# Two of the up weights' four sums, and the first four sums of each pair of values, made by GpSimd instead of VectorE

## The chip, the cores and the metric

The kernel runs on one core of one Trainium2 chip. The core has TensorE (PE, matmuls, with a row of its own for weight loads, PEld), VectorE (DVE), ScalarE (ACT), GpSimd (POOL) and SyncE (SP, which here issues the DMAs). All engines run their own instruction stream in a fixed order and wait for each other by semaphores. The metric is the device time of one execution in microseconds; lower is better.

## The reference

One layer of an encoder over 16 learned meta tokens and 256 tokens (L = 272) of width 2048, all in float32. The layer has an input projection, two groups of attention heads, an output projection with a residual, and a gated MLP with 5632 inner columns. The change touches the MLP alone:

```python
def conv_glu(x, w_gate, w_up, conv_w, conv_b, w_down):
    g = x @ w_gate
    u = x @ w_up
    gp = jnp.pad(g, ((0, 0), (pad, pad), (0, 0)))
    gc = conv_b
    for i in range(CONV_W):
        gc = gc + conv_w[i] * gp[:, i:i + L]
    return (jax.nn.silu(gc) * u) @ w_down
```

`x` is the normalised hidden state. Meta tokens are dropped at the end, so the up product and the down product need 256 tokens only, and the gate product 258.

## The kernel before

**Products in three.** The matmuls run on float32 data rounded to a shorter form (fp32r). To keep the precision, every operand is split into a high part and a low part: `hi` is the rounded value, `lo` is the difference. A product is then the sum of three matmuls: hi by hi, hi by lo, lo by hi (lines 605 to 608 for most weights, line 278 for the products of the scheme below). Weights come from HBM in pieces of up to 128 x 1024 (`raw`, five tiles and a sixth, `more_raw`, in the MLP). For each piece ACT writes the high part (`whi<-raw`, line 238) and DVE the low part (`wlo<-raw,whi`, line 242, a subtraction of two tensors). There are four `whi` and four `wlo` tiles, so the splits can be at most four pieces ahead of TensorE. `split_hi` and `split_lo` (lines 549 to 579) take the pieces in the one order in which TensorE uses them.

**The scheme of seven products.** For some blocks of the weights the kernel uses a scheme of the Strassen-Winograd kind: a product of 2 x 2 blocks from seven block products instead of eight. For the up weights this is done for six groups of four column tiles (`QUADS = (4,10,16,22,28,36)`), called quads; each needs 8 row pairs (`RowPair`), each of them one load of 128 x 1024 and four sums of its quarters of 256 columns, made in `weight_sums` (line 529): one instruction of 512 columns that makes two of them, and then two of 256, each of which needs the one before. The sums go to a second `raw` tile. A row pair has two pieces: one with raw quarters (512 + 256 columns) and one with the four sums (1024 columns). Both are split as above. The event `summed[1]`, set after the last sum, releases the split of the second piece.

**Values.** Gate tiles pass the convolution and SiLU (`gated`); `tile_up` or, for quads, `quad_out` and `quad_value` multiply the up product with the gate. `finish_value` (line 1783) splits the value for the down product. When both tiles of a pair are done, `value_sums` (line 1800) makes four sums of 128 columns in place, one after the other, then splits the result (`split_plain`: ACT high, DVE low) into the one tile `sums` and saves it by DMA to DRAM (`save_sums`); the down stage, which uses the scheme too, reads it back (`s_down<-sums` in the profile). `hl_sums` calls the same function, with a `place` or before the MLP's buffers exist (`act is None`), for sums of the hidden state. The values live in twelve tiles `mt`.

**What sets the order.** Nothing is ordered by hand. Each engine's instruction stream comes from a planner that runs when the kernel is built (`Flow`, line 111): the code is written as generators, each `yield "dve", ns` asks for an engine for a planned time, and the planner always issues the request that can start first; equal ones go by priority. Helpers give the planned times: `TT` is a tensor-tensor operation on DVE (line 240, 68 + 1.04 ns per column), `PTT` the same on POOL (line 264, 90 + 2.7 ns per column), `ACT` an activation (line 234). The planner knows of no effect of one engine on another's speed. The result is a static order for every engine, SP's DMA issues included. So a changed planned time can change the order of all that follows.

**The MLP's order of work** (`work`, lines 427 to 479): first tiles 0 to 3 plainly, then for each quad its gate tiles, the scheme's pieces mixed with the gate and up pieces of the next tiles, and the end of these. The down stage comes behind, with the scheme for half of its output columns and plain products for the others. In it POOL adds the residual (`PTT`).

Of the kernel before, what the change touches and what calls it, by code (L numbers as in the profile page):

```python
# [12 lines left out]
ALU = mybir.AluOpType  # L13
# [192 lines left out]
def encoder_block(ctx: ExitStack, tc: tile.TileContext, io):  # L206
    nc = tc.nc
# [14 lines left out]
    def size(ap):  # L222
        n = 1
        for s in ap.shape[1:]:
            n *= s
        return n
# [13 lines left out]
    def TT(out, a, b, op):  # L240
        yield "dve", 68 + 1.04 * size(out)
        nc.vector.tensor_tensor(out, a, b, op)  # L242
# [20 lines left out]

    def PTT(out, a, b, op):
        yield "pool", 90 + 2.7 * size(out)
        nc.gpsimd.tensor_tensor(out, a, b, op)  # L266

    def cost(l, r):
# [17 lines left out]
    def meta_copies(row, lo, n=P):  # L286

        out = row[:n, L : L + 3 * CW].rearrange("p (i x) -> p i x", i=3)[:, :, :N_META]
        src = row[:n, SEQ:L]
        his = out[:, :2] if lo == 2 else out[:, ::2]  # L290
        yield from ACT(his.bitcast(F32R), repeated(src, 2), AF.Copy)
        yield from PTT(out[:, lo].bitcast(F32R), src, out[:, 0], ALU.subtract)
# [4 lines left out]
    def one(slots):  # L297
        (t,) = yield slots, 1
        return t
# [141 lines left out]
    for w, f in enumerate(QUADS):  # L441
# [6 lines left out]
        for i in range(KC // 2):  # L448
            r = RowPair(io["w_up_s"][w][i], i, PW // 4)
# [7 lines left out]
        for i, u in enumerate(scheme):  # L457
            a, b = (j * len(middle) // len(scheme) for j in (i, i + 1))
# [9 lines left out]
    for g in range(FC // 2):  # L468
        r = RowPair(io["w_down_s"][g], g, PW // 2)
# [34 lines left out]
    def load_pair(r):  # L504
        if r.of == "up":
            r.raw, r.sums = yield raws, 2
        else:
            r.raw = yield from one(quarters)
        def load_S():
            if r.near:  # L510
                r.ev_S = ev_near[r.g]
                return
            r.S = yield from one(s_parts)
            src, saved = saved_sums[r.of][r.g]
            yield saved
            yield "sp", 600
            load(r.S, src, r.ev_S, nc.sync)

        if r.of == "up":
            yield from load_S()  # L520
        for a in range(0, 4 * r.q, PW):
            yield "sp", 600
            ev = r.loaded if a + PW == 4 * r.q else Event()
            load(r.raw[:, a : a + PW], r.src[:, a : a + PW], ev, nc.sync)
        if r.of == "down":
            yield from load_S()
        fl.spawn(weight_sums(r), (lambda: 0) if r.of == "up" else 2)

    def weight_sums(r):
        yield r.loaded  # L530
        if r.of == "down":
            r.sums = yield from one(sums4)
        t, raw, q = r.sums, r.raw, r.q
        yield from TT(t[:, : 2 * q], raw[:, q : 3 * q], raw[:, : 2 * q], ALU.subtract)
        fl.set(r.summed[0])
        yield from TT(t[:, 2 * q : 3 * q], raw[:, 2 * q : 3 * q], t[:, :q], ALU.subtract)
        yield from TT(t[:, 3 * q :], t[:, 2 * q : 3 * q], raw[:, 3 * q :], ALU.subtract)
        fl.set(r.summed[1])
        r.used("raw")

# [359 lines left out]
    def rope(t, n, out, tmp):  # L900

        half = ROPE // 2
        for i in range(P // half):
            yield "sp", 600
            j = i ^ 1
            swapped = Event()
            load(tmp[i * half : (i + 1) * half, :n], t[j * half : (j + 1) * half], swapped, nc.sync)
        yield from PTT(out, t, const("cos", n), ALU.mult)
        yield swapped
        yield from TT(tmp[:, :n], tmp[:, :n], const("sin", n), ALU.mult)  # L910
        yield from PTT(out, out, tmp[:, :n], ALU.add)
# [67 lines left out]
    for h in range(HEADS):  # L979
        t = apool.tile([P, 2, NT], F32R, name=f"ob{h}")  # L980
        ob.append((t[:, 0, :], t[:, 1, :]))
        t = apool.tile([P, 2, NT], F32R, name=f"oa{h}") if h < 6 else hl[KC - HEADS + h]
# [6 lines left out]
    def split_plain(hi, lo, src):  # L989
        yield from ACT(hi, src, AF.Copy)  # L990
        yield from TT(lo, src, hi.bitcast(F32), ALU.subtract)
# [734 lines left out]
    act = mts = None  # L1726
# [56 lines left out]
    def finish_value(f, u):  # L1783
        fl.put(mts, gates[f])
        u_ = u[:, :SEQ]
        if f >= FC - KC:
            yield ev_far[(f - FC + KC) // 2]
        yield from ACT(act[:, f, 0, :], u_, AF.Copy)
        yield from TT(act[:, f, 1, :], u_, act[:, f, 0, :].bitcast(F32), ALU.subtract)
        fl.set(ev_act[f])  # L1790
        values[f] = u
        if f ^ 1 in values:
            yield from value_sums(
                *saved_sums["down"][f // 2], *(values[i][:, :SEQ] for i in (f & ~1, f | 1))
            )
            for i in (f & ~1, f | 1):
                fl.put(mts, values[i])

    values = {}
    def value_sums(dst, saved, a, b, place=None):  # L1800

        (A11, A21), (A12, A22) = ((t[:, :P], t[:, P:SEQ]) for t in (a, b))

        yield from TT(A22, A21, A22, ALU.add)
        yield from TT(A21, A11, A21, ALU.subtract)
        yield from TT(A11, A22, A11, ALU.subtract)
        yield from TT(A12, A12, A11, ALU.subtract)
        parts = place
        if place is None:
            parts = yield from one(combined)  # L1810
        hl_ = parts.bitcast(F32R).rearrange("p (i t) -> p i t", i=4)
        for i, t in enumerate((a, b)):
            yield from split_plain(hl_[:, i], hl_[:, 2 + i], t)
        fl.spawn(save_sums(dst, saved, parts, place is None))

    def save_sums(dst, saved, parts, release):
        yield "sp", 600
        load(dst, parts, saved, nc.sync)
        fl.cur.t = saved.time
        if release:  # L1820
            fl.put(combined, parts)
# [4 lines left out]
    def hl_sums():  # L1826
        for i in range(KC // 2):
            for k in (2 * i, 2 * i + 1):
                yield ev_h[k]
            if i >= EARLY:  # L1830
                yield ev_mlp
            v = yield from one(raws)
            ab = [v[:, j * SEQ : (j + 1) * SEQ] for j in range(2)]
            for k, t in zip((2 * i, 2 * i + 1), ab):
                yield from ACT(t, hT[k][:, :SEQ], AF.Copy, scale=vec("g_ffn", k))
            fl.set(ev_gained[i])
            yield from value_sums(*saved_sums["up"][i], *ab, near[i])
            if i >= EARLY:
                fl.set(ev_near[i])
            fl.put(raws, v)  # L1840
# [370 lines left out]
```

## Time and profile before

| | |
|---|---|
| runs, median (lowest to highest) | 1108.89 us (1108.64 to 1109.74) |
| profiled execution: span, first to last instruction | 1106.7 us |
| PE busy | 1100.6 us, 99% |
| weight loads busy | 1061.8 us, 96% |
| DVE busy | 990.8 us, 90% |
| ACT busy | 735.1 us, 66% |
| POOL busy | 140.0 us, 13% |
| clock of TensorE granted | 1.000 |
| moved by DMA | 239.41 MB, 216 GB/s on the mean |

The profiled execution has no time of its own beside its span; what lies around the span is seen only as its distance to the runs' median. The gate and up stage lies between about 394 and 870 us of the span, the down stage behind it.

How to read the rows. A row of instructions in order of time begins with the start and the duration in us, then engine, line, operation, the tile written, an arrow, the tiles read, the shapes, and a count; in brackets stands how long the engine had been idle and what ended it. A row of a group ends with busy time in us and the mean duration in ns, and after the bar the idle time in front of the group's instructions. Reported durations of consecutive DVE instructions overlap by some hundredths of a microsecond. Matmuls are pipelined: a matmul of 258 columns is shown as 0.28 us long, while the next starts 0.12 us after it.

### The profile page before, as it was taken

The numbers are of one execution on the slowest core, as the hardware profiler recorded it, in microseconds if no ns is written. First come the engines' busy times: TensorE is split into PE (matmuls) and PEld (weight loads), VectorE is DVE, ScalarE is ACT, GpSimd is POOL, SyncE is SP. The second block draws the span as 40 slices with busy tenths as digits, with TensorE's granted clock in tenths as the row PEclk, the third lists the DMA queues.
The fourth block names the chain that finished last, engine by engine and source line by source line (L and its number), as shares of the span: only waits on it lengthen the run. The fifth ranks groups of instructions, "written<-read, shape, count | busy, mean of one in ns | idle before, by whom it ended". The sixth has DMA issues, their size and how long they took to land.

```text
span 1106.7 us, 22544 instructions
## 1 busy us (share of the span) xinstructions
PE 1100.6 (99%) x8414; PEld 1061.8 (96%) x8414; DVE 990.8 (90%) x1837; ACT 735.1 (66%) x1470; POOL 140.0 (13%) x202
## 2 busy tenths in 40 slices
PE   9999999999999999999999999999999999999998
PEld 9999999999999999999999999999999988888888
DVE  8979888888878989999999999988988999999984
ACT  8788979798647776656666565665565565655663
POOL 3211222121433400000000000000000011100114
PEclk9999999999999999999999999999999999999999
DMA  9553434444665796657667577777688787777772
GB/s 323 199 172 124 148 127 151 139 163 134 230 188 161 207 343 229 198 181 243 224 193 230 179 248 241 238 229 244 203 275 299 260 299 250 251 258 266 281 249 77
DMA packets 72374, 239.41 MB, mean 216 GB/s; under 512 B 8136, under 2 KB 12744, under 8 KB 72264
## 3 DMA queue, kind: packets, MB, share of 16 engines
q1 hardware_dynamic: 71976, 237.69, 63.8%
q8 instruction: 66, 1.08, 0.4%
q14 instruction: 44, 0.36, 0.1%
q10 hardware_dynamic: 288, 0.27, 0.1%
HBM read 219.44 MB, written 17.83 MB: 214 GB/s over the span
## 4 chain that ended last, share of the span: by engine, by line
PE 90%; ACT 4%; DVE 3%; issue 1%; DMA 1%; POOL 0%; DVEq 0%; POOLq 0%; ACTq 0%
PE bank L278 24%; PE bank L606 18%; PE bank L607 18%; PE bank L608 18%; PE bank L1870 6%; PE bank L1871 3%; PE bank L284 2%; ACT whi L238 1%; ACT scr L238 1%; DVE wlo L242 1%; DVE scr L250 1%; DMA raw<-in_w_cq 1%; ACT qraw L238 0%; ACT bank L238 0%; DVE cols L258 0%
## 5 line engine op out<-in xcount | busy, mean ns | idle before, releaser
L238 ACT ACTIVATE whi<-raw 128x512 fp32r<-128x512 f32 (+2 forms) x479 | 358.1, 764 | 173.2 <-PE bank L607 83.5
L242 DVE TENSOR_TENSOR wlo<-raw,whi 128x512 fp32r<-128x512 f32 (+2 forms) x479 | 414.9, 885 | 43.2 <-ACT whi L238 42.1
L606 PE MATMUL bank<-hl,whi 128*128 128x258 f32 (+2 forms) x1528 | 438.5, 287 | 0.1
L607 PE MATMUL bank<-hl,whi 128*128 128x258 f32 (+2 forms) x1528 | 433.7, 284 | 0.0
L608 PE MATMUL bank<-hl,wlo 128*128 128x258 f32 (+2 forms) x1528 | 433.0, 283 | 0.2 <-DVE wlo L242 0.2
L608 PEld LDWEIGHTS bank<-hl,wlo 128*128 128x128 f32 x1528 | 290.1, 190 | 0.9 <-DVE wlo L242 0.7
L607 PEld LDWEIGHTS bank<-hl,whi 128*128 128x128 f32 x1528 | 289.6, 190 | 0.1
L606 PEld LDWEIGHTS bank<-hl,whi 128*128 128x128 f32 x1528 | 288.6, 189 | 0.5 <-ACT scr L238 0.3
L238 ACT ACTIVATE whi<-quarters 128x1024 fp32r<-128x1024 f32 x88 | 81.5, 950 | 64.8 <-PE bank L1870 46.0
L278 PE MATMUL bank<-whi,act 128*128 128x256 f32 (+1 forms) x420 | 111.5, 317 | 0.0
L1870 PE MATMUL bank<-act,whi 128*128 128x512 f32 x308 | 110.1, 397 | 0.0
L242 DVE TENSOR_TENSOR wlo<-quarters,whi 128x1024 fp32r<-128x1024 f32 x88 | 99.4, 1156 | 10.8 <-ACT whi L238 10.2
L266 POOL TENSOR_TENSOR mt<-mt,mt 128x256 f32<-128x256 f32 x7 | 6.8, 979 | 652.4 <-ACT mt L238 652.4
L1871 PE MATMUL bank<-act,wlo 128*128 128x256 f32 x308 | 86.4, 281 | 0.0
L278 PE MATMUL bank<-whi,sin 128*128 128x512 f32 (+1 forms) x272 | 83.5, 355 | 0.0
L278 PEld LDWEIGHTS bank<-whi,act 128*128 128x128 f32 x420 | 74.1, 189 | 5.7
L1870 PEld LDWEIGHTS bank<-act,whi 128*128 128x128 f32 x308 | 57.8, 188 | 13.9
L278 PE MATMUL bank<-whi,hl 128*128 128x256 f32 x288 | 66.5, 280 | 0.0
L278 PE MATMUL bank<-wlo,act 128*128 128x256 f32 (+1 forms) x210 | 66.3, 315 | 0.0
L238 ACT ACTIVATE whi<-more_raw 128x1024 fp32r<-128x1024 f32 (+2 forms) x46 | 44.1, 962 | 24.4 <-PE bank L607 9.9
L1871 PEld LDWEIGHTS bank<-act,wlo 128*128 128x128 f32 x308 | 58.1, 189 | 1.6
L278 PEld LDWEIGHTS bank<-whi,sin 128*128 128x128 f32 x272 | 49.5, 188 | 7.7
(278 smaller groups left out, 1947.9 us busy)
## 6 DMA issues: line engine op xcount, KB each, us to landing
raw<-in_w_gate SPq DMA_DIRECT2D x83, 512.0 KB, 5.0
raw<-in_w_in SPq DMA_DIRECT2D x52, 512.0 KB, 3.9
raw<-in_w_up_s SPq DMA_DIRECT2D x44, 512.0 KB, 4.9
quarters<-in_w_down_s SPq DMA_DIRECT2D x44, 512.0 KB, 6.9
raw<-in_w_up SPq DMA_DIRECT2D x34, 512.0 KB, 5.5
raw<-in_w_out SPq DMA_DIRECT2D x32, 512.0 KB, 4.0
raw<-in_w_down SPq DMA_DIRECT2D x32, 512.0 KB, 5.2
s_down<-sums SPq DMA_DIRECT2D x22, 512.0 KB, 4.1
```

The costliest lines, as they stand in the source:

```text
L238: nc.scalar.activation(out, in_, f, **kw)
L242: nc.vector.tensor_tensor(out, a, b, op)
L250: nc.vector.scalar_tensor_tensor(out, a, s, b, op0, op1)
L266: nc.gpsimd.tensor_tensor(out, a, b, op)
L278: nc.tensor.matmul(o, l, r, start=start, stop=stop)
L284: nc.tensor.transpose(o, i, ident[:n, :n])
L606: nc.tensor.matmul(ps, whi, xhi, start=start, stop=False)
L607: nc.tensor.matmul(ps, whi, xlo, start=False, stop=False)
L608: nc.tensor.matmul(ps, wlo, xhi, start=False, stop=stop)
L1870: nc.tensor.matmul(ps, whi, x, start=start, stop=False)
L1871: nc.tensor.matmul(ps[:, :n], wlo, x[:, 0, :], start=False, stop=stop)
```

## The change

`SLOW` is a new helper: a tensor-tensor operation on POOL, planned at 150 + 4.1 ns per column. It is used at two places. In `weight_sums` the second and the third instruction (256 columns each) go to POOL where the row pair is one of the up weights; the first (512 columns) stays on DVE, and the down weights' sums stay on DVE. In `value_sums` the four sums of 128 columns go to POOL where they are sums of values (the MLP's `act` exists and no `place` is given); the sums of the hidden state stay on DVE. That is 48 row pairs x 2 and 22 value pairs x 4 instructions. Nothing that is computed changes.

```diff
+    def SLOW(out, a, b, op):
+        yield "pool", 150 + 4.1 * size(out)
+        nc.gpsimd.tensor_tensor(out, a, b, op)
+
...
         yield from TT(t[:, : 2 * q], raw[:, q : 3 * q], raw[:, : 2 * q], ALU.subtract)
         fl.set(r.summed[0])
-        yield from TT(t[:, 2 * q : 3 * q], raw[:, 2 * q : 3 * q], t[:, :q], ALU.subtract)
-        yield from TT(t[:, 3 * q :], t[:, 2 * q : 3 * q], raw[:, 3 * q :], ALU.subtract)
+        sub = SLOW if r.of == "up" else TT
+        yield from sub(t[:, 2 * q : 3 * q], raw[:, 2 * q : 3 * q], t[:, :q], ALU.subtract)
+        yield from sub(t[:, 3 * q :], t[:, 2 * q : 3 * q], raw[:, 3 * q :], ALU.subtract)
         fl.set(r.summed[1])
...
-        yield from TT(A22, A21, A22, ALU.add)
-        yield from TT(A21, A11, A21, ALU.subtract)
-        yield from TT(A11, A22, A11, ALU.subtract)
-        yield from TT(A12, A12, A11, ALU.subtract)
+        op = TT if act is None or place is not None else SLOW
+        yield from op(A22, A21, A22, ALU.add)
+        yield from op(A21, A11, A21, ALU.subtract)
+        yield from op(A11, A22, A11, ALU.subtract)
+        yield from op(A12, A12, A11, ALU.subtract)
```

## The prediction

> **What bounds the kernel now.** I read the page first, then busy time by stretches of the gate and up stage, then what TensorE waits for there, and last single instructions in order of time. The page:
>
> ```profile
> span 1106.7 us, 22544 instructions
> ## 1 busy us (share of the span) xinstructions
> PE 1100.6 (99%) x8414; PEld 1061.8 (96%) x8414; DVE 990.8 (90%) x1837; ACT 735.1 (66%) x1470; POOL 140.0 (13%) x202
> ```
>
> The terms below are laid against this execution, whose span is 1106.7 us. The shown runs have a median of 1108.89 us, 2.2 us more, and I add the change to that median. The stage cut at the ends of its six quads (a quad is the four up tiles that one scheme makes; I call the stretch from one to the next a round):
>
> ```profile
> 433.20:500.00 66.80, 66.80 (x562) 66.80 (x562) 61.45 (x110) 40.51 (x61) 0.00 (x0) 1.00 0.62 203
> 500.00:566.90 66.90, 66.90 (x563) 66.90 (x562) 64.24 (x120) 41.33 (x66) 0.00 (x0) 1.00 0.65 213
> 566.90:633.70 66.80, 66.80 (x561) 66.80 (x561) 64.05 (x120) 41.09 (x66) 0.00 (x0) 1.00 0.66 213
> 633.70:700.60 66.90, 66.90 (x563) 66.90 (x562) 64.20 (x123) 40.88 (x65) 0.00 (x0) 1.00 0.70 228
> 700.60:790.50 89.90, 89.90 (x755) 89.90 (x754) 80.02 (x144) 52.88 (x82) 0.00 (x0) 1.00 0.72 236
> 790.50:868.00 77.50, 77.50 (x650) 77.50 (x649) 69.27 (x120) 47.68 (x72) 0.00 (x0) 1.00 0.79 272
> ```
>
> The columns are the stretch, its length, then busy time of PE, weight load, DVE, ACT and POOL, the clock, and the DMA share. PE is never idle, and rounds of one shape take the same time and the same number of matmuls. POOL does nothing. DVE is busy 64.2 of 66.9 us, 2.7 us idle. That PE's busy time is no artefact of pipelining shows in what its groups waited for between 400 and 860 us:
>
> ```profile
> L606 PE MATMUL bank<-hl,whi 128*128 128x258 f32 (+1 forms) x934 | 264.7, 283 | 0.0
> L607 PE MATMUL bank<-hl,whi 128*128 128x258 f32 (+1 forms) x935 | 264.5, 283 | 0.0
> L608 PE MATMUL bank<-hl,wlo 128*128 128x258 f32 (+1 forms) x935 | 263.5, 282 | 0.0
> ```
>
> So the stage is bound by TensorE. DVE's work is hidden, however near to full it is. But it is hidden narrowly. A weight piece is usable when DVE has written its `wlo`; I set the end of that against the first matmul that reads it and call the distance the lead. The first and the last of the eight pieces of the stage with a lead under 0.5 us, and between them one that a weight sum holds up:
>
> ```profile
> 510.29 1.22 DVE L242 TENSOR_TENSOR wlo<-raw,whi 128x1024 fp32r<-128x1024 f32 x1
> ```
> ```profile
> 511.94 0.28 PE L608 MATMUL bank<-hl,wlo 128*128 128x258 f32 x1
> ```
> ```profile
> 517.15 1.06 ACT L238 ACTIVATE whi<-raw 128x1024 fp32r<-128x1024 f32 x1 [3.26 <-DVE raw L242]
> ```
> ```profile
> 517.69 0.42 DVE L242 TENSOR_TENSOR more_raw<-raw,more_raw 128x256 f32<-128x256 f32 x1
> 518.15 0.42 DVE L242 TENSOR_TENSOR more_raw<-more_raw,raw 128x256 f32<-128x256 f32 x1
> 518.49 1.22 DVE L242 TENSOR_TENSOR wlo<-raw,whi 128x1024 fp32r<-128x1024 f32 x1
> ```
> ```profile
> 520.08 0.28 PE L278 MATMUL bank<-wlo,act 128*128 128x256 f32 x1
> ```
> ```profile
> 716.75 1.23 DVE L242 TENSOR_TENSOR wlo<-raw,whi 128x1024 fp32r<-128x1024 f32 x1 [1.17 <-ACT whi L238]
> ```
> ```profile
> 718.29 0.28 PE L608 MATMUL bank<-hl,wlo 128*128 128x258 f32 x1
> ```
>
> The leads are 511.94 - (510.29 + 1.22) = 0.43, 520.08 - (518.49 + 1.22) = 0.37 and 718.29 - (716.75 + 1.23) = 0.31 us. At 517.15 ACT had stood idle 3.26 us for the last sum of a row pair: the work that now goes to POOL lies on the path with no slack.
>
> **The change, part by part.** *What leaves DVE.* The groups of round 500 to 566.9, two sums for each of 8 row pairs and four for each of 3 value pairs:
>
> ```profile
> L242 DVE TENSOR_TENSOR raw<-raw,raw 128x256 f32<-128x256 f32 x8 | 3.4, 421 | 0.2
> ...
> L242 DVE TENSOR_TENSOR mt<-mt,mt 128x128 f32<-128x128 f32 x9 | 2.4, 282 | 0.0
> ...
> L242 DVE TENSOR_TENSOR more_raw<-more_raw,raw 128x256 f32<-128x256 f32 x4 | 1.7, 421 | 0.1
> L242 DVE TENSOR_TENSOR more_raw<-raw,more_raw 128x256 f32<-128x256 f32 x4 | 1.7, 419 | 0.0
> ...
> L242 DVE TENSOR_TENSOR mt<-mt 128x128 f32<-128x128 f32 x3 | 0.8, 282 | 0.0
> ```
>
> That is 3.4 + 1.7 + 1.7 = 6.8 us for 16 sums of 256 columns and 2.4 + 0.8 = 3.2 us for 12 of 128: 10.0 us of a round. By itself this is worth nothing, since no matmul waits for DVE; it could pay only as longer leads.
>
> *What it costs to have POOL run beside DVE.* The stage shows no POOL, so the price is from the output projection, where it adds tensors of 258 columns: two POOL instructions and two DVE instructions of one form, the first DVE one beside POOL, the second alone; then a POOL one that met DVE at work, and the narrow form:
>
> ```profile
> 324.71 0.74 POOL L266 TENSOR_TENSOR res<-res,scr 128x258 f32<-128x258 f32 x1 [4.01 <-DVE scr L242]
> ```
> ```profile
> 324.88 1.11 DVE L242 TENSOR_TENSOR wlo<-raw,whi 128x512 fp32r<-128x512 f32 x1
> ```
> ```profile
> 325.41 1.09 POOL L266 TENSOR_TENSOR res<-res,scr 128x258 f32<-128x258 f32 x1
> ```
> ```profile
> 326.97 0.68 DVE L242 TENSOR_TENSOR wlo<-raw,whi 128x512 fp32r<-128x512 f32 x1
> ```
> ```profile
> 350.94 3.09 POOL L266 TENSOR_TENSOR kr<-kr,scr 128x258 f32<-128x258 f32 x1 [4.29 <-ACT scr L238]
> ```
> ```profile
> L266 POOL TENSOR_TENSOR p<-p 128x16 fp32r<-128x16 f32 x40 | 13.1, 330 | 52.9 <-ACT p L238 44.7 <-PE bank L607 3.5 <-PE bank L608 3.5
> ```
>
> The two engines hold each other up: DVE's 0.68 became 1.11 us, 0.43 lost to one POOL sum; POOL's 0.74 became 1.09, and 3.09 where DVE went on without a gap. A sum of 256 thus frees 0.42 us of DVE and takes up to 0.43 back. For 128 columns no POOL row exists. Its DVE loss lies between 0 (POOL runs in DVE's idle time) and 0.43; I take 0.43 x 128/258 = 0.21, by width. Per round: 16 x 0.43 + 12 x 0.21 = 6.9 + 2.5 = 9.4 us against 10.0 freed; with both ends, 0 to 12.0. DVE is as full as before: the relief is taken back by the contention. With 12.0 it would be 64.2 + 2.0 = 66.2 of 66.9, still not over.
>
> The Trainium skill, page "SBUF — State Buffer", section "SBUF: two separate sides", says that GpSimd and a DVE instruction with two SBUF inputs share a port pair under an exclusive lock, held for the whole instruction. The trace agrees that they exclude each other, but only 0.43 of POOL's 0.74 us was lost. The sum by the rule is that of the second rival.
>
> *The longer chain.* The second and third sum depend on each other, and the ACT split of the sums piece waits for the third. On DVE, back to back, they took 518.15 + 0.42 - 517.69 = 0.88 us. On POOL they take 2 x 0.74 = 1.48 if free, 0.74 + 1.09 = 1.83 if they alternate with DVE, 2 x 3.09 = 6.18 if DVE starves both. I take 1.83, since at 96% of DVE's time a free POOL is the exception and two starved sums another: 0.95 us later. Where DVE itself put splits between the sums POOL may instead be earlier. Behind the waiting split on ACT are the next pieces' splits, in a fixed order, and behind DVE's `wlo` of that piece all its later work; so 0.95 us reaches the next pieces, and the lead pays for it. Eight pieces have leads of 0.31 to 0.43, 3.1 us together: 8 x 0.95 - 3.1 = 4.5 us of TensorE stall. Sixteen more lie between 0.72 and 1.16; those under 0.95 give 1.4 us. Sum 5.9. Ends: 0 (relief and delay cancel), and 48 row pairs x 0.95 = 45.6 us if no lead covered any of it.
>
> *Value sums.* A 128-wide POOL sum, between 0.33 and 0.74 us by the rows for 16 and 258 columns, is about 0.33 + 0.41 x 112/242 = 0.52; a chain of four 2.1 us against 4 x 0.28 = 1.1. What hides it is that these parts are saved for the down stage; the extra 1.0 us holds ACT's split of the sums, two `mt` tiles and the single `sums` tile. The save is a DMA in SP's order with loads behind it:
>
> ```profile
> 565.21 0.33 SPq L488 DMA_DIRECT2D s_down<-sums  x1
> 565.58 0.43 SPq L488 DMA_DIRECT2D raw<-in_w_up_s  x1
> ```
>
> The next load goes out 0.37 us behind the save, so a save late by 1.0 us makes it late too. I take 0 for it, as DVE is freed at the same place by 3.2 us a round; if that cover is gone it is 1 us for each of the 6 rounds, within the range. No DMA is added or removed. The planner prices the new sums at 150 + 4.1 ns per column, so all queues behind them are ordered anew, and it does not know that DVE is slowed; it can gain no more than TensorE's idle time in the stage, which rounds to 0.0, and lose some single waits of the 3.26 us kind. I take 0, since TensorE's order of products is fixed, and leave both to the range.
>
> Sum: 1108.9 + 5.9 = 1114.8, say 1115 us.
>
> **The rivals.** *First, no stall: not slower.* The chain starts on POOL as soon as the first sum is done, where DVE now has other splits in between (the 3.26 us wait), and the chain's 0.95 us is met by DVE's 10.0 freed before its 9.4 is taken back. It decides if the chain is later by less than the 0.4 us of the tightest leads. Time: 1108.9, 1108 to 1111. For it: the balance on DVE is within 1 us; against: the tight pieces lie just in the scheme, where POOL works.
>
> *Second, the lock is the bound.* If each POOL sum takes its whole duration from DVE, a round loses 16 x 0.74 + 12 x 0.52 = 18.1 us against 10.0, and the surplus 8.1 exceeds the 2.7 idle by 5.4; the stage is 434.8 / 66.9 = 6.5 rounds, so +35, 1144 us. If all idle time of the six stretches (434.8 - 403.2 = 31.6) could be used it is 6.5 x 8.1 - 31.6 = +21, 1130 us. For it: the 3.09 row, and leads near zero; against: the 0.43 row. This is where the skill's rule named above leads.
>
> *Third, faster.* It needs matmul waits to remove. TensorE's gaps in the stage round to 0.0, so only the way into the down stage and its new order of loads could give more than 0.2%. Time about 1106.
>
> **How the numbers follow.** 0.2% (2.2 us) is about what a measurement of this kernel can tell from no change. Local stalls, 1111.2 to 1126: 0.48. No stall: 0.27. Lock-bound, over 1126: 0.20. Faster by more: 0.05. So slower 0.68, same 0.27, faster 0.05. The range 1108 to 1138 leaves out the faster case, the lower edge of the second and the upper third of the lock case. The likeliest case's own range is 1111 to 1126.
>
> **What would show it.** In the profile after: POOL busy about 16 x 0.74 + 12 x 0.52 = 18 us a round or more, with sums over 1 us; DVE's 1024-wide `wlo` longer than 1.22 on the mean, and DVE's busy time in the rounds about as before, with 10 us less of sums; the rounds longer than 66.9 us, with PE idle behind `wlo`, at row pairs' sums pieces; ACT's wait for a weight sum put down to POOL. Wrong if the rounds stay at 66.9 (first rival), if DVE's busy time falls by 5 us or more a round (no contention), or if rounds grow by 4 us or more (second).

## The result, and the profile after

The changed kernel takes 1111.42 us (1111.09 to 1112.19, 13 runs) where the kernel before takes 1109.12 (1108.44 to 1109.74, 13 runs, on the same chip): a ratio of 1.0022 with a 95% interval of 1.0014 to 1.0031. It is slower by 2.3 us. The prediction was 1115 us, slower by 5.9.

The head of the page of the changed kernel:

```profile
span 1109.5 us, 22685 instructions
## 1 busy us (share of the span) xinstructions
PE 1102.0 (99%) x8414; PEld 1062.6 (96%) x8414; DVE 982.7 (89%) x1653; ACT 733.2 (66%) x1470; POOL 346.3 (31%) x386
```

The span has grown by 2.8 us. POOL is busy 206 us longer, DVE 8 us less. With the same sums made by nobody (relief alone, below) DVE is busy 48 us less between 400 and 870 us (387.4 instead of 435.4), so most of what was taken off DVE has come back as longer instructions. The PE groups of the changed kernel between 400 and 860 us (lines 611 to 613 are the former 606 to 608):

```profile
L611 PE MATMUL bank<-hl,whi 128*128 128x258 f32 (+1 forms) x927 | 262.7, 283 | 0.0
L612 PE MATMUL bank<-hl,whi 128*128 128x258 f32 (+1 forms) x927 | 262.3, 283 | 0.0
L613 PE MATMUL bank<-hl,wlo 128*128 128x258 f32 (+1 forms) x927 | 261.9, 283 | 1.7 <-DVE wlo L242 1.7
```

TensorE, which had waited for nothing here, now waits 1.7 us for DVE's `wlo`. This is three waits, one in each of three rounds. A modelled matmul end hides part of each, so the starts tell more. The first one, in the order of PE's instructions, and the DVE instruction that it waited for:

```profile
511.84 0.29 PE L612 MATMUL bank<-hl,whi 128*128 128x258 f32 x1
512.66 0.39 PE L613 MATMUL bank<-hl,wlo 128*128 128x258 f32 x1 [0.53 <-DVE wlo L242]
```
```profile
511.39 1.22 DVE L242 TENSOR_TENSOR wlo<-raw,whi 128x1024 fp32r<-128x1024 f32 x1
```

512.66 - 511.84 = 0.82 us from one start to the next, where 0.12 is usual: a loss of 0.70. The `wlo` ends at 512.61; its lead is 0.05 us, and so it was exactly this piece that held TensorE. Counted in PE's order, the matmul at 512.66 is the 4194th of 8414, and the 4194th of the kernel before is the one at 511.94, for which the prediction read a lead of 0.43 us. The matmuls of the other two stalls started there at 578.79 and 645.65, with leads of 0.42 and 0.43. With two smaller slips in the same round (0.11 us each) the loss is 0.92 us, and three rounds make 2.8, the whole growth of the span. The other rounds lose nothing.

POOL's sums in the stage, by form (the mean duration in ns is the second number behind the bar), and the longest of them:

```profile
L270 POOL TENSOR_TENSOR raw<-raw,raw 128x256 f32<-128x256 f32 x70 | 99.1, 1415 | 173.4 <-DVE raw L242 139.4 <-ACT whi L238 25.3 <-DMA raw<-in_w_gate 6.3
L270 POOL TENSOR_TENSOR mt<-mt,mt 128x128 f32<-128x128 f32 x64 | 54.8, 867 | 53.6 <-DVE act L242 52.1
```
```profile
511.61 5.48 POOL L270 TENSOR_TENSOR raw<-raw,raw 128x256 f32<-128x256 f32 x1 [3.88 <-DVE raw L242]
```

A thing that came late in front of the stalls shows best in the second of the three rounds: SP's save of a value pair and the load just ahead of it, and ACT's next instruction on the `sums` tile.

```profile
568.75 0.33 SPq L492 DMA_DIRECT2D raw<-in_w_gate  x1
```
```profile
s_down<-sums SPq DMA_DIRECT2D x1, 512.0 KB, 5.0
```
```profile
574.46 0.42 ACT L238 ACTIVATE sums<-mt 128x256 fp32r<-128x256 f32 x1 [2.99 <-DMA s_down<-sums]
```

The save goes out at 569.35, 4.1 us later than in the kernel before (565.21), and the second row is the DMA view's line for it: 5.0 us to landing. There is one `sums` tile, so the split of the next pair can begin only when the save has landed, at 574.38. ACT stood for 2.99 us in front of that split. Its stream is in a fixed order: the weight splits behind it, which could have run, stood too. In the kernel before no such split waited in this round.

That this wait is what made the `wlo` late can't be read from the trace. DVE, which writes the `wlo`, never came to rest in front of the first stall (columns as in the prediction: length, PE, PEld, DVE, ACT, POOL):

```profile
490.30:512.60 22.30, 21.83 (x183) 21.62 (x181) 22.30 (x37) 14.68 (x27) 15.23 (x18) 1.00 0.51 173
```

DVE was busy for all of these 22.30 us, so in this order an earlier `whi` would not have made the piece earlier. What set its time is what stands in front of it in DVE's stream, and how long each of these instructions takes beside POOL. One of them stands just ahead of the piece:

```profile
510.79 0.68 DVE L242 TENSOR_TENSOR raw<-raw 128x512 f32<-128x512 f32 x1
```

Nor is the save the only thing that ACT waits for. Between 394 and 870 us it waited 7.1 us for saves by the profile's count, and for POOL's row sums more than that:

```profile
ACT whi L238 <- POOL raw L270: 30.3, 13, 3.5
```

### The profile page after: what moved, and what is told of

It is laid out like the page before. It is cut to its first block, busy times and chain, and to the rows that moved or that the text cites. A ratio compares the mean times of both kernels' runs of the same rounds, so it can differ in the third digit from the quotient of the medians.

```text
span 1109.5 us, 22685 instructions
## 1 busy us (share of the span) xinstructions
PE 1102.0 (99%) x8414; PEld 1062.6 (96%) x8414; DVE 982.7 (89%) x1653; ACT 733.2 (66%) x1470; POOL 346.3 (31%) x386
## 4 chain that ended last, share of the span: by engine, by line
PE 87%; DVE 6%; ACT 3%; DMA 2%; issue 1%; POOL 0%; DVEq 0%; SPq 0%; ACTq 0%; POOLq 0%
PE bank L282 22%; PE bank L613 18%; PE bank L611 18%; PE bank L612 18%; PE bank L1876 6%; PE bank L1877 3%; DVE wlo L242 3%; PE bank L288 2%; ACT whi L238 1%; DVE scr L250 1%; ACT scr L238 1%; DMA raw<-in_w_up_s 1%; DMA raw<-in_w_cq 1%; DVE raw L242 0%; DVE sums L242 0%
## 5 line engine op out<-in xcount | busy, mean ns | idle before, releaser
L242 DVE TENSOR_TENSOR wlo<-raw,whi 128x512 fp32r<-128x512 f32 (+2 forms) x472 | 442.7, 955 | 55.8 <-ACT whi L238 54.2
L270 POOL TENSOR_TENSOR raw<-raw,raw 128x256 f32<-128x256 f32 x70 | 99.1, 1415 | 173.4 <-DVE raw L242 139.4
L270 POOL TENSOR_TENSOR mt<-mt,mt 128x128 f32<-128x128 f32 x66 | 56.9, 873 | 53.8 <-DVE act L242 52.1
L242 DVE TENSOR_TENSOR wlo<-more_raw,whi 128x1024 fp32r<-128x1024 f32 (+2 forms) x53 | 54.7, 1041 | 2.5 <-ACT whi L238 1.4
```

## The experiments

Each is timed in several rounds beside the kernel before, on one chip for each group of four. Three theories: A, a value pair's save is late and ACT waits for it at the head of its queue; B, the row pairs' sums come late from POOL (the prediction's step); C, the lock between DVE and POOL as such.

| run | median, us | ratio to before, 95% |
|---|---|---|
| changed kernel | 1111.42 | 1.0022 [1.0014, 1.0031] |
| values only | 1111.09 | 1.0020 [1.0011, 1.0028] |
| rows only | 1110.43 | 1.0013 [1.0004, 1.0022] |
| all, save planned later | 1111.20 | 1.0024 [1.0015, 1.0033] |
| all, price doubled | 1126.49 | 1.0158 [1.0145, 1.0172] |
| rows only, save planned later | 1109.35 | 1.0003 [0.9994, 1.0012] |
| values only, save planned later | 1109.16 | 1.0003 [0.9994, 1.0011] |
| all, chain cut, save planned later | 1108.63 | 0.9997 [0.9989, 1.0006] |
| relief alone | 1109.02 | 1.0001 [0.9992, 1.0010] |
| all, chain cut | 1111.27 | 1.0021 [1.0011, 1.0030] |
| all, measured price, save planned later | 1111.04 | 1.0019 [1.0010, 1.0028] |
| all, price doubled, save planned later | 1123.75 | 1.0132 [1.0116, 1.0147] |
| before, save planned later | 1108.83 | 1.0000 [0.9991, 1.0010] |

**One half of the change at a time.** Values only:

```diff
-        sub = SLOW if r.of == "up" else TT
+        sub = TT
```

> Only the values' sums are made by GpSimd; the row pairs' sums are back on VectorE. Three theories. A, the late save: a value pair's parts are saved late, the single sums tile comes free late, and ScalarE, in order, waits about 3 us for it with weight splits behind. B, the row pairs' chain: the split of the sums piece waits for GpSimd's third sum (the prediction's step). C, the lock: VectorE is slowed by GpSimd as a whole. A expects the three stalls of about 0.9 us to stay, 1110.5 to 1112 us where before has 1109.1. B expects no stall, 1108.7 to 1109.5. C expects a loss by the number of columns, 88 x 128 of 35840, about a third of 2.3 us: 1109.9.

Rows only:

```diff
-        op = TT if act is None or place is not None else SLOW
+        op = TT
```

> Only the row pairs' sums are made by GpSimd; the values' sums are back on VectorE. A expects no stall, 1108.7 to 1109.5 us. B expects the whole loss, 1111 to 1112. C expects two thirds of it, about 1110.6.

Either half alone costs nearly as much as both: 2.3 and 1.6 us, which do not add up to 2.3. No theory had expected that of both halves; B is wrong on the values, A's expectation for the rows is missed, and C, which comes close for the rows (1110.6), is missed for the values (1109.9). Both runs stall at the same three matmuls as the changed kernel. The trace of each has the wait, ACT's at the `sums` tile, first with the values' sums on POOL, then with the rows':

```profile
507.16 0.42 ACT L238 ACTIVATE sums<-mt 128x256 fp32r<-128x256 f32 x1 [2.52 <-DMA s_down<-sums]
```
```profile
510.01 0.42 ACT L238 ACTIVATE sums<-mt 128x256 fp32r<-128x256 f32 x1 [1.49 <-DMA s_down<-sums]
```

With the values' sums back on DVE the save waits still; only shorter. So the save is late in the new order of instructions whichever half brings that order about. With the rows on POOL the wait reaches DVE just in front of the piece that held TensorE:

```profile
510.46 0.43 DVE L242 TENSOR_TENSOR sums<-mt,sums 128x256 fp32r<-128x256 f32 x1 [0.69 <-ACT sums L238]
```

With the values on POOL it doesn't, in the first and the third stall: there DVE was idle for at most 0.04 us at a time in the 22 us in front of them, as in the changed kernel.

**The wait for the save taken away.** In `save_sums` the planner believes that the tile is free when the load model says so. Told that it comes 3 us later, it orders ACT's weight splits ahead of the next pair's split, and DVE's order changes with it:

```diff
-        fl.cur.t = saved.time
+        fl.cur.t = saved.time + 3000.0
```

> The changed kernel, but the planner is told that the sums tile comes free 3 us later than it believed, so it places the next pair's split on ScalarE behind the weight splits that are ready, not in front of them. Nothing else is changed. A expects ScalarE's 3 us waits in front of the values' split to go and with them the stalls: 1109 to 1110 us. B and C expect no change from the changed kernel, 1111 to 1112.

ACT's waits of 3 us are gone, the loss is not: 1111.20. The stalls are in another place. PE, ACT and POOL of this run:

```profile
531.43 0.29 PE L612 MATMUL bank<-hl,whi 128*128 128x258 f32 x1
532.38 0.39 PE L613 MATMUL bank<-hl,wlo 128*128 128x258 f32 x1 [0.66 <-DVE wlo L242]
```
```profile
517.83 1.06 ACT L238 ACTIVATE whi<-raw 128x1024 fp32r<-128x1024 f32 x1 [3.51 <-POOL raw L270]
```
```profile
512.98 4.01 POOL L270 TENSOR_TENSOR raw<-raw,raw 128x256 f32<-128x256 f32 x1 [4.68 <-DVE raw L242]
```

Now B is seen. One row sum took 4.01 us, since DVE went on with two-input instructions of its own; ACT waited 3.51 us for its successor, and DVE stood idle for ACT:

```profile
518.92 1.23 DVE L242 TENSOR_TENSOR wlo<-raw,whi 128x1024 fp32r<-128x1024 f32 x1 [2.53 <-ACT whi L238]
```

From there on DVE had no rest; the lead was used up and TensorE lost 0.83 us at 532, and again in two further rounds. A alone is refuted as the cause of all, and so is B: each stands ready behind the other. C, which expected 1111 to 1112 too, is not excluded by this run.

**Each half with the wait for the save taken away**, and the control, the same line in the kernel before:

> Only the row pairs' sums on GpSimd, and the planner told that the sums tile comes free 3 us later. In the run with the row pairs' sums alone, ScalarE waited 1.4 to 1.6 us at the head of its queue for a save's landing, and TensorE stalled about 0.6 us behind it in three rounds. A, the late save, expects those waits and stalls to go: 1108.7 to 1109.5 us. B, the row pairs' chain, expects the loss of 1.6 us to stay: 1110 to 1111.

> Only the values' sums on GpSimd, and the planner told that the sums tile comes free 3 us later. A expects the waits of 2.4 to 3.1 us in front of the values' split to go, and with them the stalls: 1108.7 to 1109.5 us against 1111.1 without the edit. B has no row pairs' chain here to put a loss down to, and expects 1108.7 to 1109.5 with or without the edit.

> A control: the kernel before, with only the planner's belief changed (the sums tile free 3 us later). Nothing waits for a save in the kernel before, so it should be the same: 1108.5 to 1109.3 us. A gain here would mean that the edit helps by something else than the waits.

1109.35, 1109.16 and 1108.83 us: as A expects. With one half on POOL, planning the save later is enough, and nothing measurable is left. In the rows' run ACT still waits up to 3.5 us for a row sum, and no matmul stalls behind it. The control gains nothing, so the line does not help by itself. What its expectation says of the kernel before is not quite so: there ACT waits for a save four times after 700 us, for at most 1.3 us, and nothing stalls.

**The row chain cut.** The split of a row pair's second piece reads the first two sums twice and so does not wait for POOL, which makes the other two all the same:

```diff
-                pair.loaded if kind == "raw" else pair.summed[a + n > 2 * pair.q]
+                pair.loaded if kind == "raw" else pair.summed[pair.of_down and a + n > 2 * pair.q]
...
+            if kind == "sums" and not self.pair.of_down:
+                hi, lo = (x and x[:, t].rearrange("p (i c) -> p i c", i=2) for x in (self.hi, self.lo))
+                return repeated(src[:, : n // 2], 2), hi, lo
```

> All the sums on GpSimd as in the changed kernel, the planner told that the sums tile comes free 3 us later, and the row pairs' chain cut: the split of a row pair's second piece reads the first instruction's two sums twice, and so waits for VectorE's sum alone; GpSimd makes the other two sums and nobody but the next load into their tile waits for them (part of the up product is thereby left out). A and B together: with the late save alone taken away the stalls had moved to 531, 599 and 667 us, behind a wait of 3.5 us for GpSimd's row sums; with the chain cut too they go: 1108.7 to 1109.7 us. C, the lock by itself, expects the loss to stay at 1110.5 or more, as GpSimd does the same work beside VectorE.

> The changed kernel with only the row pairs' chain cut (the second piece is split from the first two sums, so part of the up product is left out); the planner's belief about the save is left as it is. With both causes taken away it was 1108.6 us, with the late save alone taken away 1111.2. A, the late save, is left: ScalarE's waits of about 3 us in front of the values' split stay and TensorE stalls near 512, 580 and 647 us: 1110 to 1111.5. If the row chain were the whole cause: 1108.5 to 1109.3.

With both edits the change costs nothing (1108.63), although POOL does all of its work beside DVE. With the chain alone cut the loss is what it was (1111.27), with ACT's waits of 3.0 to 3.1 us for the save, at the same three matmuls. So with all the sums on POOL either the save as it was planned or the row chain is enough for the loss, and without both it is gone. C falls as a cause by itself: the same work beside DVE costs nothing in another order. The order on DVE is what the trace shows to differ. In the run with both edits the same piece ends at 511.45 instead of 512.61:

```profile
510.23 1.22 DVE L242 TENSOR_TENSOR wlo<-raw,whi 128x1024 fp32r<-128x1024 f32 x1
511.36 0.42 DVE L242 TENSOR_TENSOR sums<-mt,sums 128x256 fp32r<-128x256 f32 x1
511.70 0.68 DVE L242 TENSOR_TENSOR raw<-raw 128x512 f32<-128x512 f32 x1
512.30 0.42 DVE L242 TENSOR_TENSOR sums<-mt,sums 128x256 fp32r<-128x256 f32 x1
```

The two splits of a value pair and a row pair's first sum stand behind the piece here, 1.52 us together; in the changed kernel, and with the chain alone cut, the like stand in front of it (in the changed kernel at 507.30, 508.54 and 510.79). That is enough for the 1.16 us between the two ends. That the planned order on DVE, and not ACT's wait as such, makes the first stall of the changed kernel is read from the traces; no run changed one without the other.

**Relief alone.** The sums are left out; DVE has 10 us a round less by the prediction's count, and POOL does nothing.

> VectorE's relief without GpSimd: the row pairs' second and third sum and the values' four sums are made by nobody, and the second piece of a row pair is split from the first two sums (so part of the up product and of the sums for the down product is left out). It prices the first term of the prediction, that the 10 us a round taken off VectorE are by themselves worth nothing: 1108.7 to 1109.3 us. If TensorE had been waiting for VectorE in a way that the profile hides, it would be faster, 1107 or less.

1109.02 us: a DVE with more room is worth nothing here. But room makes a late save harmless: ACT waits for one in this run too, in the second round, and TensorE loses only 0.27 us behind it and nothing in the other rounds:

```profile
573.64 0.42 ACT L238 ACTIVATE sums<-mt 128x256 fp32r<-128x256 f32 x1 [3.22 <-DMA s_down<-sums]
```

This run and the one with both edits also price the contention, since TensorE sets the pace of both. Round 500 to 566.9, relief alone first, then the same sums on POOL (columns as before: length, PE, PEld, DVE, ACT, POOL):

```profile
500.00:566.90 66.90, 66.90 (x563) 66.90 (x562) 56.56 (x92) 41.86 (x65) 0.00 (x0) 1.00 0.64 213
```
```profile
500.00:566.90 66.90, 66.90 (x563) 66.90 (x562) 64.94 (x92) 41.95 (x65) 33.37 (x29) 1.00 0.65 213
```

DVE runs 92 instructions in both, for 56.56 and for 64.94 us: POOL's 29 sums take 8.4 us of DVE's time. In the kernel before DVE was busy 64.24 us, so in this order the sums cost DVE as much on POOL as on itself. In the changed kernel they cost it less. One of its longer rounds, again with 92 instructions of DVE and 29 sums:

```profile
568.00:635.80 67.80, 67.27 (x563) 66.98 (x562) 62.50 (x92) 40.91 (x65) 35.10 (x29) 1.00 0.63 210
```

62.50 - 56.56 = 5.9 us are taken back there, and 64.24 - 62.50 = 1.7 us of the round stay free.

**The planner's price.** First doubled:

```diff
-        yield "pool", 150 + 4.1 * size(out)
+        yield "pool", 300 + 8.2 * size(out)
```

> The changed kernel with the planned price of a GpSimd sum doubled (300 + 8.2 ns per column: 2.4 us for 256 columns, 1.35 for 128, above the measured means of 1.4 and 0.9 us). A expects the values' splits to be planned late enough that ScalarE does not wait at their head: 1109 to 1110.5 us. B expects no gain, as the chain itself is as long as it was: 1111 to 1112. C expects 1111 to 1112 too.

> The run with the doubled price took 1126.5 us, where 1109 to 1112 was expected; in it ScalarE waited 4.3 to 4.8 us for a save's landing in four rounds. If those waits made its loss, telling the planner that the tile comes free 3 us later takes most of it away: 1109 to 1113 us. If it is the doubled price's own order (later loads, later row sums), it stays above 1120.

The first was missed by all three theories (1126.49 us). For the second, 1123.75 us is what its other alternative said, that the doubled price's own order makes the loss. With the doubled price ACT's waits for saves rose to 22.8 us in the stage, in the view of waits:

```profile
ACT sums L238 <- DMA s_down<-sums: 22.8, 8, 4.8
```

With the save planned later three of these waits are still there (2.8 to 4.1 us), and another one is seen that the prediction had named and priced at 0: SP's stream, in which a load of a row pair stands behind a save, and the sum that waited for its landing.

```profile
512.92 0.33 SPq L492 DMA_DIRECT2D raw<-in_w_gate  x1
513.59 0.33 SPq L492 DMA_DIRECT2D s_down<-sums  x1
514.01 0.38 SPq L492 DMA_DIRECT2D raw<-in_w_up_s  x1
```
```profile
519.95 0.69 DVE L242 TENSOR_TENSOR raw<-raw 128x512 f32<-128x512 f32 x1 [0.35 <-DMA raw<-in_w_up_s]
```
```profile
522.71 0.39 PE L282 MATMUL bank<-wlo,act 128*128 128x256 f32 x1 [0.82 <-DVE wlo L242]
```

How the 15 us divide among these waits is not settled. They show that a price above what POOL takes is no safe side: it moves the saves and the loads behind them.

Last, the means that the changed kernel's trace gives, 331 + 4.23 ns per column, with the save planned later:

> All sums on GpSimd, computed in full, with the planner told what was measured: a GpSimd sum at 331 + 4.23 ns per column (1.41 us for 256 columns and 0.87 for 128, the means of the changed kernel), and the sums tile free 3 us later. If a plan with the right mean is enough, the stalls shrink: 1109 to 1110 us. If it is single sums held off by VectorE for 4 to 5 us, which no mean foretells, ScalarE's wait for a row sum stays and so does the loss: 1110.5 to 1111.5.

1111.04 us, no better. ACT still waits up to 3.5 us for a row sum. A mean does not help where single sums take 0.73 us and others 4.0. No version with POOL beat the kernel before, and TensorE's gaps in this stage of it leave nothing to win.

## Why the prediction was partly right, point by point

*TensorE bounds the stage, DVE's relief is worth nothing by itself:* right (relief alone, 1109.02 us).

*The balance on DVE:* right in the sum, off in both terms. I took 10.0 us a round as freed; it is 64.24 - 56.56 = 7.7, since the durations that I added overlap. I took 9.4 us as taken back; it is 5.9 in the changed kernel and 8.4 in the run with both edits. For single instructions my prices were low. Two rows of one form each, beside POOL and alone, from the changed kernel:

```profile
496.92 1.76 DVE L242 TENSOR_TENSOR wlo<-raw,whi 128x1024 fp32r<-128x1024 f32 x1
```
```profile
498.60 0.68 DVE L242 TENSOR_TENSOR sums<-mt,sums 128x256 fp32r<-128x256 f32 x1
```
```profile
508.54 0.41 DVE L242 TENSOR_TENSOR sums<-mt,sums 128x256 fp32r<-128x256 f32 x1
```

0.68 - 0.41 = 0.27 us lost to a sum of 128 columns (0.21 taken), and 1.76 - 1.22 = 0.54 us to one of 256 (0.43 taken); not every sum met DVE, so the total came out lower.

*The longer chain of row sums, 5.9 us:* this is the step that failed. It let a delay of 0.95 us strike each of 24 tight pieces. Three of the eight tightest stalled, those with leads of 0.42 to 0.43, and their `wlo` was 1.1 us late (512.61 against 511.51 in the first). The pieces of the row sums, such as the one at 520.08, did not stall, and the three stalls stay where they were with the row chain cut. A stall, once it has happened, also gives its lead to the pieces behind it: in the changed kernel ACT's wait of 3.5 us for a row sum ends at 517.9, just behind the first stall, and costs nothing, while with the save planned later, without that stall, the like was followed by a loss of 0.83 us. With the save planned later the rows alone measured 0.5 us (1109.35 against 1108.86, an interval that holds zero).

*The value sums, taken at 0:* the second half of that failure. The prediction named the single `sums` tile, ACT's split and the save in SP's order, and let DVE's relief cover them. Where DVE really is relieved it does (relief alone: a wait of 3.2 us, 0.27 us lost). But the prediction's own balance had nearly all of the relief taken back, so there was no cover to count on. In the changed kernel a save has 3 to 5 us of landing behind it, ACT's queue stands meanwhile, and DVE, full again, has values' work in front of a tight piece. Values alone measured +2.3 us, and +0.3 with the save planned later.

*The mechanism of local stalls at thin leads, in rounds, behind `wlo`:* right, with 0.9 us in each of three rounds instead of 5.9 in all, and the first stall is at the piece that the prediction showed first. What made that piece late was not the row sums' chain.

*The rivals:* "no stall" comes out with both edits, or with one half on POOL and the save planned later, not in the changed kernel. "The lock is the bound" is refuted by the run with both edits: 64.94 of 66.9 us, no stall. The page "SBUF — State Buffer" of the Trainium skill (section "SBUF: two separate sides") has the lock held for a whole instruction; here the loss to DVE was 0.54 us of a POOL sum whose shortest duration in the rows is 0.73, so the lower price was the right one. Whether a POOL sum's reported duration is the time that it holds the lock, no run here shows.

## What to carry to other kernels

On engines that execute in order, the price of moving work is not its duration but what the new order puts in front of the pieces with the thinnest lead: a wait at the head of another engine's queue, or other work on an engine without rest. Look for single buffers that a DMA must empty (here one `sums` tile) and plan their release late: the control lost nothing by it, and each half of the change was free with it. Work moved from DVE to POOL, with two inputs in SBUF on both sides, freed little of DVE's time here (8 of 48 us), since DVE was busy with the like; and when several thin margins lie behind each other, taking one wait away only shows the next, so test the causes together as well as one by one.

## What the runs showed of the hardware that was not expected

A POOL sum of 256 columns can wait far longer than one DVE instruction: it took 5.48 us at 511.61, and 4.01 us with the save planned later, against 0.73 for its successor in that run, with DVE at rest:

```profile
517.06 0.73 POOL L270 TENSOR_TENSOR raw<-raw,raw 128x256 f32<-128x256 f32 x1
```

DVE's loss stayed small: in the changed kernel's stage no DVE instruction of a form that occurs more than eight times took more than 0.56 us longer than the shortest of its form. POOL's loss went on while DVE had two-input instructions in a row: both long sums ended 0.60 us after DVE had come to rest (517.09 after 516.49, 516.99 after 516.39). And the landing of a 512 KB save differed from 3 us in the kernel before, with no load just ahead, to 5.0 us with a load issued 0.6 us before it; that the load ahead is the cause was not tested by itself.
